# Cross attention of the prompt in seven products a pair of tiles instead of eight

## The chip, the cores and the metric

The kernel runs on one core of one Trainium2 chip. The metric is the device time of one execution in microseconds (us), the median of several. TensorE is called PE here (PEld is its weight load), VectorE DVE, ScalarE ACT, GpSimd POOL and SyncE SP; the last issues most of the transfers.

## What is computed

One layer of a streaming encoder over a prompt of 2048 rows (16 tiles of 128 rows, 1024 columns) and a sample tile of 128 rows: a mixer (attention and convolution), cross attention into 256 memory tokens, and a feed-forward network (FFN). The change touches the cross attention of the prompt and what it hands to the FFN:

```
h = rmsnorm(x, g_mem_pre)
x = x + rmsnorm(memory_attention(h, mk, mv, w_mq, w_mo), g_mem_post)
h = rmsnorm(x, g_ffn_pre)

def memory_attention(h, mk, mv, w_mq, w_mo):
    q = (h @ w_mq).reshape(B, T, MEM_HEADS, MEM_HEAD_DIM)
    s = einsum("bthd,bmhd->bhtm", q, mk) * MEM_HEAD_DIM ** -0.5
    p = softmax(s, axis=-1)
    o = einsum("bhtm,bmhd->bthd", p, mv).reshape(B, T, D_MODEL)
    return o @ w_mo
```

For the prompt, the memory is the same for all rows, so an earlier stage has multiplied the weights and the memory together: `f1s` (1024 x 1024) takes a normed row straight to its 4 x 256 scores, and `f2s` (1024 x 1024) takes its 4 x 256 probabilities straight to the 1024 columns of the output.

Every product is made in three matmuls of a split format: high x high, high x low and low x high, the high part a cast by ACT to fp32r and the low part the difference, by DVE or POOL.

## The kernel before

The stages run one after the other: the memory's products, the mixer's projections, its attention, its output (`mixout`, with the sample tile's cross attention as filling work), the prompt's cross attention (`phase_cross`), gate and up of the FFN (`gate_up`), its down projection. Instructions are written out for all engines, and a scheduler that works on modelled times puts each engine's list in order, earlier code first where several are ready; `high_priority` moves code ahead and `issue_after` holds it behind another instruction. Each engine and each transfer queue then runs its list strictly in order and waits on semaphores.

On-chip memory is laid out by hand. `Region.at` and `Region.lay` give each named tile a list of places (in KB) in three arenas: `sbF` (fp32), `sbR` (fp32r, its last 20 KB appear as sbx in the profile) and `ps` (PSUM), which live for the whole program; calling for a tile again takes the next place in its list. The `flex` tiles (flexb) are taken per stage, from memory that the stage ahead has given back.

`phase_cross` before: for each of 16 tiles, `norm` loads x1, makes 1/rms (ACT square, POOL power), scales (DVE, L317), transposes eight pieces on PE (L320) and splits them (ACT L321, DVE L322). `scores` multiplies them by f1: eight pieces of 128, each six matmuls of 128 x 512 (`mm3h`, L293: three forms by two halves of the 1024 columns). Softmax reads the scores in PSUM (DVE L1282, ACT L1286, DVE L1291), `probs` transposes and splits the probabilities (PE L1297, ACT L1300, DVE L1301), and `values` multiplies them by f2 in the same way. Score tile t+1 is computed between `probs` of t and `values` of t. `postnorm` (ACT L310, DVE L341, POOL L342) adds the residual and stores x2 (POOL's queue, L343). f1 and f2 (eight pieces of 1024 columns each, in high and low parts) lie on chip side by side, loaded and split by `load` (L1261, ACT L1264, DVE or POOL L1265).

The FFN multiplies pairs of tiles by the seven-product scheme of Strassen and Winograd. `natural` prepares its left side for a pair: it loads the two x2 tiles back, norms each, makes four combinations of their halves on POOL (L1330 to L1336) and stores seven pieces to `hn` by POOL's queue. One pair is done after each tile from the fifth on, and the last one inside `gate_up`. `gate_up` starts by loading `hn` pieces of its first six tiles, transposing and splitting them (`tform`: SP L1404, PE L1407, ACT L1409, DVE L1410) and by loading and combining the first weights (`wforms`: SP L1416 and L1417, POOL L1424 to L1427, ACT L1429, DVE L1430); both have `high_priority`. Its products are L285 to L287 (`mm3`), 384 rows a matmul.

## Time and profile before

| | before |
|---|---|
| median of 3 runs | 3001.84 us (2998.27 to 3007.77) |
| the profiled execution | 3001.3 us, its span 2999.5 us |
| mean granted TensorE clock | 0.992 |
| busy: PE, DVE, ACT, POOL | 98%, 71%, 45%, 47% of the span |

The profile is of one execution. The page gives each engine's busy time; the other views are answers about the same trace. In a timeline row stand the start and the duration in us, the engine, the line of the kernel, the operation, what it writes and reads, the shape and the count of equal instructions merged; in brackets the idle time before it and what ended it. In a row of groups stand the count, the busy time, the mean ns of one, the idle time before them and its releasers. A row of a source gives the smallest, median and largest ns. In a row by stretch stand the window, its length, then for PE, PEld, DVE, ACT and POOL the busy time and the count, then the granted clock, the busy share of the DMA engines and GB/s. SPq is SP's queue.

### The profile page before, as it was taken

Reading aid. Unit: us, or ns where it says so; the run is one execution under the profiler, and the core shown is the slowest. Engines: PE = TensorE matmul, PEld = TensorE weight load, DVE = VectorE, ACT = ScalarE, POOL = GpSimd, SP = SyncE. Lnnn points to the kernel's source line nnn. Section 1 sums busy time; section 2 is a strip of 40 time slices with the busy share of each in tenths; the row PEclk is TensorE's granted clock in tenths of the full one; section 3 lists DMA queues with packets and bytes.
Section 4 is the critical chain, followed back from the end, with each engine's and each line's share of the span. In section 5 each row is a group of like instructions: output and inputs, shape, how many; then the busy total and the mean of one; then the engine's idle time right before and its main releaser. Section 6 shows DMA issues by size and latency. Waiting matters only on the chain.

```text
span 2999.5 us, 46097 instructions
## 1 busy us (share of the span) xinstructions
PE 2939.8 (98%) x16924; PEld 2710.8 (90%) x16924; DVE 2134.7 (71%) x3086; ACT 1357.9 (45%) x2729; POOL 1419.3 (47%) x1338
## 2 busy tenths in 40 slices
PE   7999999989999999999999999999999999999998
PEld 7999999989998887887888999999999999888887
DVE  6697795877786466435358888888788998555666
ACT  4545364667884344323234333433334444433433
POOL 1268396731123335235357565555555775524413
PEclk9999999989999999999999999999999999999999
DMA  8735253655444556314246333544334345756664
GB/s 285 256 114 173 98 162 113 207 195 182 160 146 165 178 189 207 122 69 143 96 152 229 120 137 113 195 161 156 136 131 155 140 144 195 256 186 206 221 230 149
DMA packets 197694, 500.09 MB, mean 167 GB/s; under 512 B 19349, under 2 KB 84765, under 8 KB 188627
## 3 DMA queue, kind: packets, MB, share of 16 engines
q1 hardware_dynamic: 182539, 427.53, 42.0%
q0 software_dynamic: 14928, 69.61, 6.2%
q8 instruction: 133, 2.18, 0.3%
q14 instruction: 94, 0.77, 0.1%
HBM read 365.97 MB, written 141.81 MB: 169 GB/s over the span
## 4 chain that ended last, share of the span: by engine, by line
PE 38%; DMA 3%; DVE 3%; issue 3%; POOL 2%; ACT 1%; SPq 0%; DVEq 0%; POOLq 0%; ACTq 0%
PE psb L287 12%; PE psb L286 12%; PE psb L285 12%; DMA sbf<-in_w_down_dram 2%; PE psb L293 2%; POOL sbf L1552 1%; DMA sbf<-x 1%; PE psb L1407 1%; DVE sbr L1622 0%; DMA sbf<-hn 0%; DVE sbr L1430 0%; DVE sbr L1556 0%; POOL sbf L342 0%; DVE sbx L1430 0%; DVE flexb L1492 0%
## 5 line engine op out<-in xcount | busy, mean ns | idle before, releaser
L285 PE MATMUL psb<-sbr 128*128 128x384 f32 (+3 forms) x2808 | 942.4, 337 | 4.8 <-DVE flexb L430 2.1
L286 PE MATMUL psb<-sbr 128*128 128x384 f32 (+3 forms) x2356 | 807.1, 343 | 3.6 <-DVE sbr L322 3.3
L287 PE MATMUL psb<-sbr 128*128 128x512 f32 (+3 forms) x1848 | 633.2, 344 | 3.5 <-DVE sbr L1622 3.4
L285 PEld LDWEIGHTS psb<-sbr 128*128 128x128 f32 x2808 | 531.1, 189 | 34.7 <-DVE flexb L430 2.9
L287 PE MATMUL psb<-sbr,sbx 128*128 128x384 f32 (+2 forms) x1484 | 477.9, 323 | 0.0
L286 PEld LDWEIGHTS psb<-sbr 128*128 128x128 f32 x2356 | 446.0, 189 | 30.5 <-DVE sbr L322 3.6
L287 PEld LDWEIGHTS psb<-sbr 128*128 128x128 f32 x1848 | 348.1, 189 | 33.4 <-DVE sbr L1622 6.4
L293 PE MATMUL psb<-sbr 128*128 128x512 f32 x1200 | 295.0, 394 | 3.6 <-DVE flexb L1060 1.9
L1430 DVE TENSOR_TENSOR sbr<-sbf,sbr 128x512 fp32r<-128x512 f32 x258 | 262.4, 1020 | 39.9 <-ACT sbr L1429 39.1
L1429 ACT CAST sbr<-sbf 128x512 fp32r<-128x512 f32 x258 | 159.2, 620 | 279.1 <-PE psb L286 224.0
L287 PEld LDWEIGHTS psb<-sbr,sbx 128*128 128x128 f32 x1484 | 281.7, 190 | 0.2
L527 DVE SCALAR_TENSOR_TENSOR psb<-sbf,psb 128x768 f32<-128x768 f32 (+1 forms) x290 | 264.5, 912 | 6.1
L293 PEld LDWEIGHTS psb<-sbr 128*128 128x128 f32 x1200 | 222.1, 189 | 49.0 <-DVE flexb L1060 2.3
L1622 DVE TENSOR_TENSOR sbr<-sbf,sbr 128x384 fp32r<-128x384 f32 (+2 forms) x242 | 168.9, 721 | 96.1 <-ACT sbr L1621 93.5
L280 POOL TENSOR_TENSOR sbx<-sbf,sbr 128x1024 fp32r<-128x1024 f32 x62 | 157.6, 2545 | 78.3 <-ACT sbr L279 74.7
L1621 ACT CAST sbr<-sbf 128x384 fp32r<-128x384 f32 (+2 forms) x242 | 112.5, 483 | 171.6 <-PE psb L286 148.0
L1552 POOL TENSOR_TENSOR sbf<-sbf 128x512 f32<-128x512 f32 x77 | 106.9, 1392 | 166.6 <-DMA sbf<-in_w_down_dram 164.6
L537 POOL TENSOR_TENSOR flexb<-flexb,flexb 128x128 f32<-128x128 f32 (+1 forms) x180 | 169.2, 941 | 22.4 <-ACT flexb L536 11.8
L285 PE MATMUL psb<-sbr,sbx 128*128 128x384 f32 (+1 forms) x524 | 170.6, 327 | 0.7 <-ACT sbr L1409 0.7
L1429 ACT CAST sbx<-sbf 128x512 fp32r<-128x512 f32 x153 | 94.7, 620 | 160.8 <-PE psb L286 145.9
L1430 DVE TENSOR_TENSOR sbx<-sbf,sbx 128x512 fp32r<-128x512 f32 x153 | 154.9, 1014 | 15.1 <-ACT sbx L1429 14.8
L1424 POOL TENSOR_TENSOR sbf<-sbf 128x512 f32<-128x512 f32 x66 | 97.6, 1479 | 107.6 <-DVE sbr L1430 50.7
(345 smaller groups left out, 6257.4 us busy)
## 6 DMA issues: line engine op xcount, KB each, us to landing
af<-flexb SPq DMA_DIRECT2D x33, 1344.0 KB, 5.6
sbf<-in_w_down_dram SPq DMA_DIRECT2D x154, 256.0 KB, 3.5
sbf<-in_w_gate_dram SPq DMA_DIRECT2D x66, 512.0 KB, 3.3
sbf<-in_w_up_dram SPq DMA_DIRECT2D x66, 512.0 KB, 3.6
sbf<-af SPq DMA_DIRECT2D x85, 384.0 KB, 4.0
sbf<-x SPq DMA_DIRECT2D x49, 512.0 KB, 3.9
sbf<-in_w_in_dram SPq DMA_DIRECT2D x48, 512.0 KB, 4.0
sbr<-ks POOLq DMA_DIRECT2D x16, 1024.0 KB, 9.2
```

Source lines behind the costliest of these rows:

```text
L280: self.lo_engine.tensor_tensor(lo[:, :], wf[:, :], hi[:, :].bitcast(F32), ALU.subtract)
L285: nc.tensor.matmul(ps, lh, rh, start=start, stop=False, **kw)
L286: nc.tensor.matmul(ps, lh, rl, start=False, stop=False, **kw)
L287: nc.tensor.matmul(ps, ll, rh, start=False, stop=stop, **kw)
L293: nc.tensor.matmul(y[o], l, r[:, o * 512:(o + 1) * 512], start=start and x == 0, stop=stop and x == 2)
L527: nc.vector.scalar_tensor_tensor(acc if w < CW - 1 else o, src(w), cwt[:, j, w:w + 1], acc, ALU.mult, ALU.add)
L537: nc.gpsimd.tensor_tensor(o, o, v, ALU.add)
L1429: nc.scalar.copy(hs[j][:, :], src[j])
L1430: nc.vector.tensor_tensor(ls[j][:, :], src[j], hs[j][:, :].bitcast(F32), ALU.subtract)
L1552: nc.gpsimd.tensor_tensor(acc[:, :], acc[:, :], q[:, :], ALU.add if s > 0 else ALU.subtract)
L1621: nc.scalar.copy(ch[:, m], a[:, x, m])
L1622: nc.vector.tensor_tensor(cl[:, m], a[:, x, m], ch[:, m].bitcast(F32), ALU.subtract)
```

## The change

`phase_cross` is written anew, with the seven-product scheme for the cross attention too. The prompt's 16 tiles make eight pairs (the pairs that the FFN uses). There are 16 passes: eight over the pairs with f1 (scores), then eight with f2 (values). A pass is four rounds, one for each piece of 128 of the contracted half; a round makes seven products of three matmuls of 128 x 512 each, into seven PSUM banks that collect over the four rounds. `left` brings a pair's two tiles: for the scores it loads and norms x1, for the values it loads the probabilities, which the score passes now store in memory (`zs`). `turned` transposes four pieces for a round two rounds ahead, makes four small combinations (128 x 128), and splits seven pieces at once (896 columns) into `row`, a flex tile. `side` loads the two halves of f1 or f2 for one round's index, makes four combinations and splits seven pieces. There is room for one factor alone: f2 replaces f1 piece by piece during the eighth pass. `collect` evicts the seven banks into two tiles by one ACT copy and seven DVE additions.

After a score pass, softmax runs on the collected tiles, its scaling on POOL. After a value pass, `residual` norms and adds x1 (loaded a second time) and stores x2 for the end of the kernel; then `ffn_norm` and `natural` make the FFN's combinations straight from the tiles on chip, and their stores go through SP's queue. The sample pair is done at the start of the fourth pass (round 12); nothing is left for `gate_up`. In `mixout` two small areas change places (`sh`).

```diff
+        pool = (Region().lay(sbF, 0, ("g", 4, 2), ("z", 4, 4), ("ft", 2, 4)).lay(sbF, 0, ("g", 4, 2), ("y", 4, 4), ("x1", 4, 2))
...
+                .at("row", 7, *[(rows[i], [0]) for i in (1, 2, 3, 0)]))
...
+        ps_mm = ps_t = Region().at("mm", 2, (self.ps, [0, 2, 4, 6, 8, 10, 12])).at("t", 2, (self.ps, [14]))
...
+        def side(src, k):
...
+            b11, b12, b21, b22 = raw
+            t1, t3, t2, t4 = [self.t(pool, [P, 512], F32, "ft")[:, :] for _ in range(4)]
+            ptt(t1, b12, b11, ALU.subtract)
+            ptt(t3, b22, b12, ALU.subtract)
+            tt(t2, b22, t1, ALU.subtract)
+            tt(t4, t2, b21, ALU.subtract)
+            out = {}
+            for i, (j, x) in enumerate(((0, b11), (4, t1), (2, b21), (6, b22), (3, t3), (1, t2), (5, t4))):
+                hi = self.t(pool, [P, 512], F32R, f"fh{k}{i}")[:, :]
+                nc.scalar.copy(hi, x)
+                lo = self.t(pool, [P, 512], F32R, f"fl{k}{i}")[:, :]
+                tt(lo, x, hi.bitcast(F32), ALU.subtract)
+                out[j] = (hi, lo)
+            return out
...
+        def turned(ab, k, q):
...
+            pt = self.t(ps_t, [P, 4, P], F32, "t")
+            for i, (x, kk) in enumerate(((b, k), (a, k), (a, k + 4), (b, k + 4))):
+                nc.tensor.transpose(pt[:, i, :], x[:, kk * P:(kk + 1) * P], self.ident[:, :])
+            g = self.t(pool, [P, 8, P], F32, "g")
+            nc.scalar.copy(g[:, :4, :], pt[:, :, :])
+            b0, a0, a1, b1, s1, s2, s3, s4 = (g[:, i, :] for i in range(8))
+            other = ptt if q < 8 else tt
+            ptt(s1, b0, b1, ALU.add)
+            other(s3, a0, b0, ALU.subtract)
+            ptt(s2, s1, a0, ALU.subtract)
+            other(s4, a1, s2, ALU.subtract)
+            row = self.t(pool, [P, 14, P], F32R, "row")
+            nc.scalar.copy(row[:, :7, :], g[:, 1:, :])
+            tt(row[:, 7:, :], g[:, 1:, :], row[:, :7, :].bitcast(F32), ALU.subtract)
...
+        def collect(ps, tag):
...
+            nc.scalar.copy(a0, ps[0])
+            tt(a1, a0, ps[1], ALU.add)
+            tt(b0, a1, ps[3], ALU.add)
+            tt(b1, b0, ps[4], ALU.add)
+            tt(a1, a1, ps[4], ALU.add)
+            tt(b0, b0, ps[5], ALU.subtract)
+            tt(a1, a1, ps[6], ALU.add)
+            tt(a0, a0, ps[2], ALU.add)
...
+            for h in range(MH):
+                nc.gpsimd.tensor_scalar(zv[:, h, :], zv[:, h, :], ri[:, h:h + 1], None, ALU.mult)
+            nc.gpsimd.dma_start(self.zs[t], z)
...
+        def residual(t, y, x1):
+            r = rstd(y)
+            stt(y, y, r[:, :], self.gpost[:, :], ALU.mult, ALU.mult)
+            ptt(y, y, x1[:, :], ALU.add)
+            nc.gpsimd.dma_start(self.x2[t], y)
+
+        def ffn_norm(src, dst, n=P):
+            r = rstd(src, n)
+            stt(dst, src, r[:n, :], gffn[:n, :], ALU.mult, ALU.mult)
+
+        def natural(dst, xa, xb, n=P):
...
+            ptt(u[:, 0, :], xb[:, 0, :], xa[:, 0, :], ALU.subtract)
+            nc.sync.dma_start(dst[:n, 0:2, :], xa)
+            ptt(u[:, 1, :], xb[:, 1, :], u[:, 0, :], ALU.subtract)
+            nc.sync.dma_start(dst[:n, 4:6, :], u)
+            ptt(xb[:, 0, :], xb[:, 1, :], xb[:, 0, :], ALU.subtract)
+            nc.sync.dma_start(dst[:n, 2:4, :], xb)
+            ptt(xa[:, 1, :], u[:, 1, :], xa[:, 1, :], ALU.subtract)
+            nc.sync.dma_start(dst[:n, 6, :], xa[:, 1, :])
...
+        def finish(q, ps):
+            ta, tb, g, p = pairs[q % 8]
+            if q < 8:
+                for t, z in zip((ta, tb), collect(ps, "z")):
+                    softmax(t, z)
+                return
...
+            for t in (ta, tb):
+                x1 = self.t(pool, [P, D], F32, "x1")
+                nc.sync.dma_start(x1[:, :], self.x1[t])
...
+            ys = collect(ps, "y")
+            for t, y, x in zip((ta, tb), ys, xs):
+                residual(t, y, x)
+                ffn_norm(y, x)
+            natural(self.hn[g][:, p, :, :], *xs)
...
+        for r in range(n):
+            q, k = divmod(r, 4)
+            if k == 0:
+                ps = [self.t(ps_mm, [P, 512], F32, "mm")[:, :] for _ in range(7)]
+                if q + 1 < 16:
+                    nat[q + 1] = left(q + 1)
+            if r + AHEAD < n:
+                x, kk = divmod(r + AHEAD, 4)
+                acts[r + AHEAD] = turned(nat[x], kk, x)
+            act = acts.pop(r)
+            for j in (0, 2, 6, 4, 3, 1, 5) if r == 0 else (0, 1, 3, 4, 5, 6, 2):
+                self.mm3(ps[j], *act[j], *f[k][j], k == 0, k == 3)
+            if q == 7:
+                f[k] = side(f2, k)
+                if k == 3:
+                    self.gpost = self.gain(pool, "g_mem_post", "gain")
+            if k == 3:
+                finish(q, ps)
+            if r == 12:
+                samples()
...
-                    if g == 0 and x == 1 and self.todo:
-                        self.natural(*self.todo.pop(0))
```

199 lines of the change are left out of this document (81 added, 118 removed).

## The prediction

> **What bounds the kernel now.** I read the page first, then the busy time by stretch, then the timeline of TensorE through the stage that changes.
>
> ```profile
> span 2999.5 us, 46097 instructions
> PE 2939.8 (98%) x16924; PEld 2710.8 (90%) x16924; DVE 2134.7 (71%) x3086; ACT 1357.9 (45%) x2729; POOL 1419.3 (47%) x1338
> ...
> 1196.00:1582.00 386.00, 379.55 (x1792) 314.50 (x1791) 179.96 (x194) 126.23 (x266) 154.51 (x180) 1.00 0.34 119
> ```
>
> TensorE (PE) is busy for 98% of the span. In the cross attention of the prompt (1196 to 1582) it stands idle for about 6 of 386 us, while VectorE (DVE), ScalarE (ACT) and GpSimd (POOL) are at 47%, 33% and 40%. Matmuls taken away there shorten the time as long as the other three can do what is put on them instead.
>
> ```profile
> 1190.52 1.20 PE L293 MATMUL psb<-flexb,sbx 128*128 128x512 f32 x4 [0.77 <-DVE flexb L1085]
> 1194.97 1.80 PE L320 MATMUL psb<-ident,sbf 128*128 128x128 f32 x8 [3.25 <-DVE sbr L322]
> 1196.42 7.62 PE L293 MATMUL psb<-sbr 128*128 128x512 f32 x28
> ...
> 1258.97 8.87 PE L293 MATMUL psb<-sbr 128*128 128x512 f32 x38
> ...
> 1566.63 1.03 PE L1297 MATMUL psb<-ident,sbf 128*128 128x128 f32 x8
> 1567.42 2.09 PE L293 MATMUL psb<-flexb,sbr 128*128 128x512 f32 x8
> ...
> 1582.14 0.34 PE L285 MATMUL psb<-sbr 128*128 128x384 f32 x1
> ```
>
> The last sample matmul ends near 1191.7, the first score product starts at 1196.42 and the first gate/up product at 1582.14. Inside, 38 matmuls take 8.87 us: (8.87 - 0.39) / 37 = 0.229 us from one to the next. Eight transposes take 1567.42 - 1566.63 = 0.79.
>
> **The change, part by part.** The profiled execution took 3001.3 us (1.8 around the span) and the median of the runs is 3001.84; the sum is made against 3001.3.
>
> *Matmuls.* Before: 16 tiles x 2 products x 8 pieces x 6 = 1536. After: 64 rounds x 7 products x 3 = 1344. The transposes stay 256. 192 x 0.229 = 44.0 us less. A round is 21 x 0.229 + 4 x 0.099 = 5.2 us, and a pass of four rounds over one pair of tiles 20.8.
>
> *Prices*, from sources and groups:
>
> ```profile
> L537 POOL TENSOR_TENSOR flexb<-flexb,flexb x180: 453/462/2842, 198.7 to 620.7; 128x128 f32<-128x128 f32 x120, 128x768 f32<-128x768 f32 x60
> L806 POOL TENSOR_SCALAR flexb<-flexb,flexb x4: 961/963/984, 665.9 to 863.6; 128x272 f32<-128x272 f32 x4
> L342 POOL TENSOR_TENSOR sbf<-sbf x16: 2380/2396/3412, 1241.6 to 1586.0; 128x1024 f32<-128x1024 f32 x16
> L1425 POOL TENSOR_TENSOR sbf<-sbf x66: 1282/1542/1777, 1554.2 to 2508.6; 128x512 f32<-128x512 f32 x66
> L303 POOL TENSOR_TENSOR sbf<-sbf,mhalf 128x1 f32<-128x1 f32 x28 | 15.5, 555 | 2.3
> L302 POOL TENSOR_SCALAR sbf<-sbf 128x1 f32<-128x1 f32 x28 | 5.2, 186 | 178.1 <-ACT sbf L310 178.1
> DMA to landing us min/median/max: 3.1/4.8/5.8
> L1430 DVE TENSOR_TENSOR sbr<-sbf,sbr x258: 676/693/1979, 1550.4 to 2520.6; 128x512 fp32r<-128x512 f32 x129
> L1265 DVE TENSOR_TENSOR flexb<-sbf,flexb x5: 1214/1226/1226, 1224.0 to 1233.2; 128x1024 fp32r<-128x1024 f32 x5
> L317 DVE SCALAR_TENSOR_TENSOR sbf<-sbf x16: 1271/1791/3389, 1167.0 to 1536.1; 128x1024 f32<-128x1024 f32 x16
> L1410 DVE TENSOR_TENSOR sbr<-psb,sbr 128x512 fp32r<-128x512 f32 x4 | 2.8, 690 | 6.8 <-ACT sbr L1409 6.8
> L1429 ACT CAST sbr<-sbf x258: 602/622/627, 1548.9 to 2520.0; 128x512 fp32r<-128x512 f32 x129
> ```
>
> The smallest or median durations are the undisturbed ones. VectorE between 512 and 1024 columns gains 1.05 ns a column: 0.27 for 128, 1.09 for the 896 of the low parts.
>
> *The start.* The split combinations (`row`) and the gains lie in the flex tiles, in memory that the mixer's output stage held.
>
> ```profile
> 1191.76 1.02 ACT L310 ACTIVATE flexb<-psb 128x1024 bf16<-128x1024 f32 x1 [1.60 <-PE psb L293]
> ...
> 1205.61 1.27 DVE L341 SCALAR_TENSOR_TENSOR flexb<-psb,flexb 128x1024 f32<-128x1024 f32 x1
> ...
> 1210.57 0.63 POOL L343 DMA_DIRECT2D x<-flexb  x1 [0.30 <-POOL flexb L342]
> ...
> 1214.03 0.33 SPq L364 DMA_DIRECT2D flexb<-in_g_ffn_pre_dram  x1
> ```
>
> The load of g_ffn_pre comes ahead of all f1 loads in the program, yet starts at 1214.03, 3.5 us after the sample's last store from that memory was issued: a flex tile is given over whole. Before, no score product touched one. After, the first needs `row`, and its transposes need a PSUM bank that holds the sample's y until L341. The shortest chain, from the square at 1191.76: 1.0, then 0.74 for 1/rms (L302, L303), 1.3 (L341), 2.4 (L342), 0.9 for issuing, 3.1 to land (the least of L343's), 0.9 for the copy into `row` (896 columns, between 0.62 for 512 and the square's 1.02 for 1024): 1202.1, or 6 later than 1196.42. Before lost 7.62 - 28 x 0.229 = 1.2 in its first tile, where after has its weights ready for two rounds. I take +5; if L341 runs as late as now the first product comes at about 1215 and it is +17; 0 if the conversions of f1, which pace rounds 2 and 3 either way, swallow it.
>
> [...]
>
> ```profile
> 1699.22 1.47 POOL L1522 TENSOR_TENSOR flexb<-flexb 128x384 f32<-128x384 f32 x1
> 1700.66 1.28 POOL L1425 TENSOR_TENSOR sbf<-sbf 128x512 f32<-128x512 f32 x1
> 1701.91 1.74 POOL L1426 TENSOR_TENSOR sbf<-sbf 128x512 f32<-128x512 f32 x1
> ...
> 1700.38 0.55 DVE L1483 TENSOR_TENSOR sbf<-sbf,psb 128x384 f32<-128x384 f32 x1
> 1700.85 1.65 DVE L1430 TENSOR_TENSOR sbr<-sbf,sbr 128x512 fp32r<-128x512 f32 x1
> 1702.42 1.65 DVE L1485 SCALAR_TENSOR_TENSOR flexb<-flexb,sbf 128x384 f32<-128x384 f32 x1
> ```
>
> L1483, with one operand in PSUM, runs its 0.55 beside L1522. L1430, with both inputs in SBUF, starts beside L1425 and ends 0.56 after it (2.50 against 1.94); L1426 then ends 1.15 after L1430. They take turns; only some 0.13 us of each, its issue, overlaps.
>
> [...]
>
> Score passes: POOL 16 combinations x 0.46 + 8 scalings x 0.91 (L806, at 256 columns) = 14.6; DVE with two SBUF inputs 4 x 1.09 + 2 x 1.27 = 6.9. Together 21.5 by durations, 17.6 by turns (0.13 off each of 30), of 20.8. So it fits, narrowly; the four `z` tiles give a lag of two passes. +2 (0 to 6).
>
> Value passes: POOL 8 x 0.46 + 2 residual additions x 2.39 + 4 FFN combinations x 1.28 = 13.6; DVE 4 x 1.09 + 8 x 0.27 + 4 x 1.27 = 11.6. Together 25.2 by durations and 21.3 by turns, of 20.8. POOL's own list adds four 1/rms (0.74 each) and two stores; its FFN stores move to SP, behind loads that wait for their slots. Four `y` tiles let the finishing of a pair lag by two passes, but the gate/up stage needs the space of the last `y` and `x1`, so the lag is paid at the latest there. I take 22.0 a pass, nearer to the turns, since L1430 shows turns: 7 passes x 1.2 = +8 (3 to 31).
>
> For scale, gate/up runs close to this:
>
> ```profile
> 1700.00:1900.00 200.00, 200.00 (x1155) 200.00 (x1155) 162.19 (x221) 76.56 (x139) 114.38 (x82) 1.00 0.36 128
> ```
>
> There DVE and POOL together are busy 277 of 200 us, blocked time included, and PE stands still for none of it.
>
> *The change from f1 to f2.* Four sides in rounds 29 to 35 (7 x 5.2 = 36 us). DVE: 36 x 0.69 = 24.8, low parts 7 x 1.09 = 7.6, evictions 7 x 0.69 = 4.8 (L1410's form), two maxima over 1024 columns (some 1.2 each) and six small differences: 4, an estimate: 41. ACT: 28 x 0.62 = 17.4 and its usual work, which fits. DVE is 5 over: +6 (0 to 16, with POOL's 8 x 1.28 on the port).
>
> *Into gate/up.*
>
> ```profile
> 1586.56 0.66 PE L1407 MATMUL psb<-ident,sbf 128*128 128x128 f32 x4 [0.55 <-DVE sbr L1410]
> 1590.10 1.25 PE L1407 MATMUL psb<-ident,sbf 128*128 128x128 f32 x8 [0.97 <-DVE sbr L1410]
> 1596.47 1.16 PE L1407 MATMUL psb<-ident,sbf 128*128 128x128 f32 x8 [1.73 <-DMA sbf<-hn]
> ...
> 1597.00:1602.00 5.00, 4.67 (x19) 4.04 (x19) 1.57 (x3) 1.27 (x3) 4.98 (x6) 0.66 0.74 193
> ...
> sbf<-in_w_up_dram SPq DMA_DIRECT2D x66, 512.0 KB, 3.6
> ```
>
> Before waits 3.3 us in these three, since first loads and conversions were done earlier. After, the first w_up load goes to the space of the last pair's `y`, and the first gate/up sum to its `x1`. From the last cross product: the last evictions 2, two squares 2.0, 1/rms 0.7, scaling 1.3, two additions 4.8, square and 1/rms 1.8, scaling 1.3, four combinations 5.1, store 3.1, two gate/up sums 2.6, cast 0.6: product 1 can start 25 us on. PE has products 0 and 2 (24 x 200 / 1155 = 4.2) and 84 transposes (8.3) till then: 13 idle, so +10 (0 to 20). Each such pause also costs clock: 0.66 was granted at 1597 to 1602, after the waits. [...]
>
> Sum: -44 + 5 + 2 + 6 + 8 + 10 = -13: **2988 us**.
>
> **Rivals.**
> *The cover holds.* `z`, `y` and AHEAD = 2 soak up the lag, and the last pair finishes beside the 21 transposed loads of gate/up: -44 + 5 + 2 + 3 = -34, 2967 us. For it: VectorE, ScalarE and GpSimd each stay under 20.8 a pass alone, and gate/up above. Against: the turns.
> *The port becomes the bound* (slower). Turns as costly as whole durations, 25.2 a pass: -44 + 5 + 6 + 10 + 7 x 4.4 + 10 = +18, 3019 us (6 and 10 for the score passes and f2, toward their upper ends). It also needs only GpSimd's order going wrong, 2.4 us additions ahead of 0.46 us combinations that PE waits for. It decides from 23.8 a pass, where the sum is nil. For it: 21.3 is already over 20.8. Against: two passes of slack.
> *The matmuls saved aren't worth it*: seven banks in turn might pace worse than 0.229.
>
> ```profile
> L285 PE MATMUL psb<-sbr 128*128 128x512 f32 x692 | 270.0, 390 | 0.0
> L293 PE MATMUL psb<-sbr 128*128 128x512 f32 x764 | 185.0, 393 | 1.7 <-ACT sbr L1300 1.1 <-POOL sbr L1265 0.6
> ```
>
> The seven-product form in the down stage (L285) takes 390 ns, as the pairs do (393); at 0.25 it would be 2988 + 1344 x 0.02 = 3015.
>
> **How the numbers follow.** About 0.3% (9 us) can be told from no change. The forecast 0.45, its own range 2973 to 3009 (faster 0.25, same 0.20); the cover holds 0.20, faster; the port 0.31 (slower 0.28, same 0.03); the pace 0.04 (slower 0.03, same 0.01). Faster 0.45, same 0.24, slower 0.31. Range 2962 to 3026, from the cover's price less 5 to the port's and 8 more.
>
> **What would show it.** Right: 1344 matmuls at 0.229; first product at about 1202; value passes near 22 us; POOL near 90% from the ninth pass on, with its additions and VectorE's two-input instructions above 2.4 and 1.3; a pause of 10 to 20 us ahead of gate/up's second product, ended by POOL or a load. Wrong: passes at 20.8 and no pause (the cover), passes of 24 or more with PE waiting for `row` or for evictions (the port).

## The result, and the profile after

The changed kernel takes 3156.43 us (median of 4, 3153.48 to 3160.00) where the kernel before takes 3004.81 beside it: 1.0506 times the time, 95% interval 1.0488 to 1.0524. It is slower by 152 us; 2988 had been forecast and 2962 to 3026 given as the range.

The head of the page, the stretches of the stage (busy time of PE, PEld, DVE, ACT and POOL, then granted clock, DMA share and GB/s) and TensorE's rows around them, all of the changed kernel:

```profile
span 3155.9 us, 46575 instructions
PE 2935.6 (93%) x16732; PEld 2693.6 (85%) x16732; DVE 2276.3 (72%) x3289; ACT 1445.1 (46%) x2881; POOL 1610.4 (51%) x1587
```
```profile
1213.00:1460.00 247.00, 190.06 (x800) 151.43 (x800) 138.43 (x172) 111.60 (x244) 166.97 (x237) 0.87 0.25 87
1460.00:1667.00 207.00, 182.12 (x788) 143.70 (x788) 143.56 (x177) 76.97 (x130) 137.82 (x153) 0.94 0.38 142
1667.00:1733.00 66.00, 3.16 (x13) 2.36 (x13) 23.18 (x22) 16.12 (x28) 40.37 (x41) 0.54 0.44 163
```
```profile
1213.01 0.79 PE L285 MATMUL psb<-sbr,flexb 128*128 128x512 f32 x1 [9.91 <-ACT flexb L1330]
...
1666.52 0.39 PE L287 MATMUL psb<-sbr,flexb 128*128 128x512 f32 x1
1684.43 1.12 PE L1475 MATMUL psb<-ident,sbf 128*128 128x128 f32 x4 [17.52 <-DVE sbf L1344]
1730.28 1.97 PE L1475 MATMUL psb<-ident,sbf 128*128 128x128 f32 x8 [44.74 <-DMA sbf<-hn]
1732.93 0.69 PE L285 MATMUL psb<-sbr 128*128 128x384 f32 x1 [0.68 <-ACT sbr L1477]
```

Before, TensorE was full in this stage; now no engine is. Four pieces make the 156.4 us between the two spans (3155.9 and 2999.5): the first product starts at 1213.0 for 1196.4 (+16.6); the passes take 453.7 where the stage before took 385.7 (+68.0); between the last product and the first of gate/up TensorE pauses for 66.2 us, where before there was no pause (the three waits of 3.3 us came just behind the first gate/up product); from that product on it takes 1422.9 for 1417.4 (+5.5).

For every kernel below I took the starts of the 1344 products with 512 columns (84 to a pass) and of the first gate/up product. A pass lasts from its first product to that of the next; passes 1 to 7 make scores, f2 replaces f1 in the eighth, and passes 9 to 16 make values. In us:

| kernel | ratio | first product | passes 1–7, mean | 8 | 9 | 10–16, mean | pause | gate/up on |
|---|---|---|---|---|---|---|---|---|
| after | 1.0506 | 1213.0 | 29.4 | 41.5 | 30.1 | 25.2 | 66.2 | 1422.9 |
| e1 x1 free | 1.0425 | 1219.7 | 28.7 | 41.5 | 29.2 | 25.8 | 34.9 | 1429.6 |
| e2 scaling on DVE | 1.0351 | 1218.0 | 23.1 | 33.7 | 26.6 | 24.6 | 67.6 | 1427.4 |
| e3 operands first | 1.0467 | 1221.9 | 28.9 | 38.0 | 25.9 | 23.8 | 67.1 | 1423.8 |
| e4 e1+e2+e3 | 1.0254 | 1224.8 | 22.6 | 28.8 | 32.9 | 25.4 | 35.0 | 1430.3 |
| e6 places | 1.0485 | 1219.1 | 28.6 | 41.3 | 29.7 | 25.2 | 20.5 | 1461.4 |
| e7 sums on DVE | 1.0358 | 1217.0 | 23.9 | 32.0 | 30.1 | 25.1 | 60.9 | 1425.7 |
| e8 same, from PSUM | 1.0357 | 1215.6 | 26.1 | 38.0 | 28.7 | 25.5 | 42.2 | 1428.7 |
| e9 finishing order | 1.0401 | 1214.0 | 28.7 | 41.4 | 29.7 | 25.3 | 26.3 | 1436.6 |
| e10 e9+e1+e2 | 1.0269 | 1213.2 | 23.2 | 33.4 | 26.5 | 28.0 | 21.1 | 1435.7 |
| e11 addition on DVE | 1.0173 | 1217.5 | 23.0 | 33.6 | 26.7 | 23.7 | 25.2 | 1427.2 |
| e12 scaling dealt out | 1.0410 | 1221.1 | 25.2 | 32.2 | 31.9 | 24.9 | 66.5 | 1426.7 |
| e13 | 1.0197 | 1215.5 | 23.2 | 37.4 | 30.3 | 24.4 | 16.3 | 1429.0 |
| e14 | 1.0148 | 1214.4 | 21.5 | 33.3 | 27.0 | 23.9 | 13.7 | 1438.1 |
| e15 | 1.0141 | 1210.1 | 22.0 | 39.6 | 25.8 | 22.4 | 16.3 | 1441.6 |
| e16 | 1.0143 | 1216.3 | 22.0 | 39.9 | 27.4 | 21.5 | 11.5 | 1454.1 |
| e17 no FFN sums | 1.0306 | 1220.3 | 28.6 | 41.2 | 29.7 | 22.3 | 15.9 | 1428.1 |
| e18 e15, no FFN sums | 1.0073 | 1211.6 | 22.2 | 40.1 | 25.8 | 20.9 | 7.2 | 1441.1 |

The ratios' 95% intervals reach 0.0013 to 0.0018 to either side. They are taken against the kernel before as it ran beside each (3004.0 to 3009.0 us), so small differences are read from them and not from the times. All runs but e5 are in the table.

### The profile page after: what moved, and what is told of

The parts are those of the page before. It is cut to its first block, busy times and chain, and to the rows that moved or that the text cites. A ratio compares the mean times of both kernels' runs of the same rounds, so it can differ in the third digit from the quotient of the medians.

```text
span 3155.9 us, 46575 instructions
## 1 busy us (share of the span) xinstructions
PE 2935.6 (93%) x16732; PEld 2693.6 (85%) x16732; DVE 2276.3 (72%) x3289; ACT 1445.1 (46%) x2881; POOL 1610.4 (51%) x1587
## 4 chain that ended last, share of the span: by engine, by line
PE 40%; POOL 3%; DMA 3%; issue 2%; DVE 1%; ACT 1%; POOLq 0%; SPq 0%; DVEq 0%; ACTq 0%
PE psb L287 13%; PE psb L286 13%; PE psb L285 13%; DMA sbf<-in_w_down_dram 1%; POOL sbf L1618 1%; PE psb L1475 1%; DMA sbf<-x 1%; DMA sbf<-hn 1%; POOL sbf L1364 0%; ACT sbf L1295 0%; DVE sbr L1688 0%; POOL sbf L1297 0%; POOL flexb L1377 0%; POOL sbf L1298 0%; DMA hn<-sbf 0%
## 5 line engine op out<-in xcount | busy, mean ns | idle before, releaser
L285 PEld LDWEIGHTS psb<-sbr 128*128 128x128 f32 x2808 | 530.3, 189 | 35.0 <-ACT sbr L1687 1.9
L286 PEld LDWEIGHTS psb<-sbr 128*128 128x128 f32 x2356 | 445.2, 189 | 29.7 <-DVE sbr L322 3.6
L287 PEld LDWEIGHTS psb<-sbr 128*128 128x128 f32 x1848 | 347.9, 189 | 32.9 <-DVE sbr L1688 6.1
L285 PE MATMUL psb<-sbr,flexb 128*128 128x512 f32 (+2 forms) x496 | 194.6, 392 | 66.2 <-ACT flexb L1330 63.6
L286 PE MATMUL psb<-sbr,flexb 128*128 128x512 f32 (+2 forms) x532 | 211.8, 398 | 0.0
L1618 POOL TENSOR_TENSOR sbf<-sbf 128x512 f32<-128x512 f32 x77 | 106.6, 1390 | 166.4 <-DMA sbf<-in_w_down_dram 164.8
L287 PE MATMUL psb<-sbr,flexb 128*128 128x512 f32 (+2 forms) x496 | 171.9, 374 | 4.9 <-DVE flexb L1331 4.8
L285 PEld LDWEIGHTS psb<-sbr,flexb 128*128 128x128 f32 x496 | 98.0, 198 | 84.9 <-ACT flexb L1330 68.6
```

The costliest lines, as they stand in the source:

```text
L285: nc.tensor.matmul(ps, lh, rh, start=start, stop=False, **kw)
L286: nc.tensor.matmul(ps, lh, rl, start=False, stop=False, **kw)
L287: nc.tensor.matmul(ps, ll, rh, start=False, stop=stop, **kw)
L1618: nc.gpsimd.tensor_tensor(acc[:, :], acc[:, :], q[:, :], ALU.add if s > 0 else ALU.subtract)
```

## The experiments

Two readings are set against each other. By the *lists*, what costs is the order of each engine's list: a short instruction that TensorE needs stands behind long ones. By the *port*, what costs is the sum of the durations of VectorE's instructions with two SBUF inputs and of GpSimd's, as if they had to run one after the other. The port, in the prediction and the expectations too, is a name for what these instructions wait for; what it is, no run shows. What the prediction's rows show is that they get longer beside each other: L1430 took 1.65 us beside L1425 and L1426, where its shortest took 0.68.

**Score passes: where the scalings stand.** GpSimd in the fourth pass of the changed kernel, and TensorE's wait there:

```profile
1304.88 0.46 POOL L1328 TENSOR_TENSOR sbf<-sbf 128x128 f32<-128x128 f32 x1
1308.61 7.26 POOL L1358 TENSOR_SCALAR sbf<-sbf 128x256 f32<-128x256 f32 x8 [3.27 <-DVE sbf L1356]
1315.83 0.46 POOL L1325 TENSOR_TENSOR sbf<-sbf 128x128 f32<-128x128 f32 x1
...
1322.04 1.84 POOL L1328 TENSOR_TENSOR sbf<-sbf 128x128 f32<-128x128 f32 x2
```
```profile
1324.49 0.80 PE L285 MATMUL psb<-sbr,flexb 128*128 128x512 f32 x1 [6.42 <-ACT flexb L1330]
```

GpSimd stands idle 3.3 us ahead of the scalings (their exponentials aren't done), scales for 7.3 us, and only then makes the combinations of the next rounds: 17 us from one round's L1328 to those of the next two rounds. Two rounds of lookahead are 10.4 us.

e2 takes the scalings out of that list:

```diff
-                nc.gpsimd.tensor_scalar(zv[:, h, :], zv[:, h, :], ri[:, h:h + 1], None, ALU.mult)
+                nc.vector.tensor_scalar(zv[:, h, :], zv[:, h, :], ri[:, h:h + 1], None, ALU.mult)
```


> Edit: the eight scalings of a pair's softmax (L1358, 0.9 us each on GpSimd) go to VectorE, one line. Theory of the lists: GpSimd works off its list in its written order, and the scalings (7.3 us in a row) stand there ahead of the combinations of the next rounds that TensorE waits for; with them gone from that list the score passes, 23 to 41 us now (mean 30.9 of eight), lose 3 to 6 us each from the third on: about 25 us less, 3130 us, and the combinations L1325 to L1328 of a round follow each other at once. Port theory: the same direction, by 7.3 us of the port a pass less what VectorE's scalings cost there, also some 20 to 30 us; so the two are told apart by e3, and this run only gives the price of the scalings. If neither holds and operands come late for another reason (x1 loads and 1/rms of the next pair), under 10 us are won.

3113.07 us: 43 less, and the passes not touched by f1's conversions or the samples run at 20.6 to 21.2. That fits list and port alike. e5 and e12 keep the scalings on GpSimd and deal them out, two to a round:

```diff
+                late.append(lambda h=h: nc.gpsimd.tensor_scalar(...))        # e5, e12
...
+            with self.tc.issue_after(self.last_comb.ins):                    # e12 alone: behind L1327
+                for _ in range(min(2, len(late))):
+                    late.pop(0)()
```


> Edit: the softmax scalings stay on GpSimd, as many and as long as before, but are written two to a round into the four rounds of the next pass, behind that round's combinations, instead of sixteen... eight after another per tile at the end of a pass. Moving them to VectorE won 43 us (ratio 1.035 for 1.051) and brought the score passes from 30.9 to 24.4 us in the mean. Theory of the lists: what costs is that combinations stand behind a block of scalings that itself waits for the exponentials (GpSimd idled up to 7.6 us ahead of a block in e1); dealt out, they cost little: score passes of 22 to 25 us, 3115 to 3130 us in all. Port theory: the work on the shared port is the same, 21.5 us by durations a pass, so the score passes stay near 29 to 31 and the time within 12 us of 3156.

e5 took 3159.68: the scheduler put the scalings in rows of eight as before (1311.24, 7.24 us, x8), so it tests nothing.

> Edit: what e5 meant to do and did not (its list of GpSimd came out with the eight scalings of a pair in a row as before, so e5 says nothing): here two scalings are made to follow a round's combination on GpSimd. Engines, work and durations are those of the changed kernel. Theory of the lists: score passes from 30.9 in the mean to 22 to 25, 3110 to 3130 us in all, near e2. Port theory: 21.5 us of port work a pass by durations as before, score passes above 28, time within 12 us of 3156.

e12 took 3131.49, 25 us less, with the same work on the same engines; passes 1 to 7 fell from 29.4 to 25.2 in the mean, pass 8 from 41.5 to 32.2. TensorE's longest waits in passes 3 to 7 (us, times, longest), in the changed kernel, e12 and e2:

```profile
PE psb L285 <- ACT flexb L1330: 30.0, 6, 8.5
...
PE psb L285 <- ACT flexb L1330: 15.4, 8, 4.5
...
PE psb L285 <- ACT flexb L1330: 6.3, 2, 3.3
```

L1330 is the cast of the split combinations. So most of what e2 won is the order of GpSimd's list; the 2 us a pass between e12 and e2 may be the port's or the list's. In pass 8 the block of scalings took even longer:

```profile
1436.63 11.19 POOL L1358 TENSOR_SCALAR sbf<-sbf 128x256 f32<-128x256 f32 x8
```

The combinations behind it came to GpSimd at 1447.8; the last one of the round (L1328, in VectorE's list) stood there behind f2's sums, low parts and evictions until 1458.7, and TensorE waited 12.1 us for the cast after it.

e3 only asks for another order:

```diff
+                    with self.tc.high_priority(offset=200):
                         nat[q + 1] = left(q + 1)
...
+                with self.tc.high_priority(offset=200):
                     acts[r + AHEAD] = turned(nat[x], kk, x)
```


> Edit: what makes the operands of coming rounds (the transposes with copy, combinations and split; and the loading and norm of the next pair) gets a higher priority (200 steps of the program) when the order of each engine's list is written; no work is added, moved to another engine or left out. Theory of the lists: the score passes get shorter, since combinations no longer stand behind scalings and squares of finished tiles: 20 to 40 us less, 3115 to 3135. The value passes stay, as the ring of the x1 tiles sets them. Port theory: the sum of the work on the port is the same, so the time stays within 10 us of 3156.

3147.84, 9 us less: not the list theory's 20 to 40, and within the 10 that the port theory allowed. But the scheduler takes whatever is ready first by its modelled times, and six of the eight blocks of eight scalings stayed whole in the list, so e3 does not decide between the two.

**The port by itself.** e7 and e8 differ in where VectorE reads:

```diff
-            ptt(s1, b0, b1, ALU.add)
+            tt(s1, b0, b1, ALU.add)                     # e7; s2, s3 and s4 likewise
+            tt(s1, pt[:, 0, :], b1, ALU.add)            # e8: one input from PSUM; s2, s3 and s4 likewise
```


> Edit: all four combinations of a round (L1325 to L1328) on VectorE, reading from SBUF as before: 0.27 us instead of 0.46 each, and none in GpSimd's list. This run and e8 are a pair: the lists of all engines are of the same kind in both, only the port differs. Port, by durations: a score pass 7.3 (scalings) + 11.2 (VectorE with two SBUF inputs) = 18.5 us; a value pass 9.9 + 13.8 = 23.7 us. Port theory: value passes stay at 24 or more, since TensorE needs 20.8. Theory of the lists: GpSimd's finishing work stands ahead of nothing that TensorE waits for; score passes 21 to 23, value passes 21 to 23, and some 60 to 90 us won: 3065 to 3095.

> Edit: as e7, but each of the four combinations takes one of its two inputs from PSUM, where the transposes left it, so that (as the one-PSUM-input evictions in the trace of before ran beside GpSimd) it need not take turns with GpSimd. Port, by durations: a score pass 14.2 us, a value pass 9.9 + 9.5 = 19.4 us. Port theory: value passes fall to 21 to 22, by 2 to 3 us each below e7, so 15 to 25 us less than e7. Theory of the lists: the same as e7 within 10 us.

3113.88 and 3113.03. In e7 the value passes stayed at 25.1, as the port theory said and the list theory (21 to 23) did not. In e8, where the port theory has them at 21 to 22, they are 25.5: the port's sum of durations does not bound these passes. The equal times hide two differences. e8's score passes are 2 us longer: 9.1 us of TensorE's waits in them end on its L1327, the last combination, which in e8 reads the one PSUM bank that the next transposes need; e7 has no such wait. And e8's pause is 18.7 us shorter, so a pair's finishing did go faster with less work on the port.

**The pause is a debt.** GpSimd's residual addition of each pair at the end of the stage:

```profile
1664.59 2.39 POOL L1364 TENSOR_TENSOR sbf<-sbf 128x1024 f32<-128x1024 f32 x1 [7.50 <-DMA sbf<-x]
...
1692.38 2.34 POOL L1364 TENSOR_TENSOR sbf<-sbf 128x1024 f32<-128x1024 f32 x1 [7.53 <-DMA sbf<-x]
...
1719.91 2.34 POOL L1364 TENSOR_TENSOR sbf<-sbf 128x1024 f32<-128x1024 f32 x1 [6.42 <-DMA sbf<-x]
```

Each row is the first addition of a pair. It waits for an x1 load, which waits for the x1 tile, which the FFN norm fills and the last of four stores gives back: 27.5 to 27.8 us a pair, all in one chain, against 20.8 for a pass. The last three passes (27.1, 27.7, 27.5) run at that period, and after the last product three pairs are still owed.

```diff
-                ffn_norm(y, x)                          # e1: the norm over y, x1 free after the addition
-            natural(self.hn[g][:, p, :, :], *xs)
+                ffn_norm(y, y)
+            natural(self.hn[g][:, p, :, :], *ys)
```


> Edit: the FFN norm of a value tile is written over y itself instead of over its x1 tile, so an x1 tile is free after the residual addition and no longer held until the four stores of the FFN combinations have landed. The work on every engine stays the same. Ring theory: in the changed kernel the residual addition (L1364) of a new pair starts every 27.5 to 27.8 us at the end of the stage, after a reload of x1 (4.2 to 5.1 us) that waits for the stores of the pair before; the value passes take on this period (27.1 to 27.7 us for the last three) and the finished pairs still owed make the 66 us pause after the last cross product. Without the ring the passes from the third value pass on fall to 21 to 23 us (some 25 us less in all) and the pause to 20 to 30 us (some 40 less): about 3090 us, ratio 1.03 to the kernel before, against 1.051. Port theory: what VectorE and GpSimd share is as full as before, so value passes stay at 25 or more and at most 15 us are won: 3140 or more.

```diff
             for t, y, x in zip((ta, tb), ys, xs):       # e9: both residuals, then both norms
                 residual(t, y, x)
-                ffn_norm(y, x)
+            for y, x in zip(ys, xs):
+                ffn_norm(y, x)
```


> Edit: the finishing of a pair of value tiles is written in another order, nothing else: first both residuals, then both FFN norms (before: residual and norm of one tile, then of the other). GpSimd's list then has the two residual additions next to each other, and ScalarE's squares of the second tile no longer stand behind the addition of the first. Theory of the finishing chain: a pair is finished in a chain of 27.7 us (from one L1364 to that of the next pair: 1664.59, 1692.38, 1719.91 in the changed kernel), longer than a pass needs (20.8), so each value pass comes to wait for the y tiles of two passes ago, and the debt of some three pairs is the 66 us pause. By the same rows the new chain is: reload 5, two additions 4.8, square 1.2, 1/rms 1.6, scaling 1.3, combinations 6, store 2.1 = 22 us. Value passes then fall from 25.8 to 22 to 23 (some 22 us less), the pause by 10 to 30: 3105 to 3125 us. Port theory: same work, same port: within 12 us of 3156.

e1: 3135.71; e9: 3129.23. Both cut the pause (to 34.9 and 26.3), as the chain theory says; neither shortened the value passes (25.8 and 25.3), which by the same theory should have fallen to 21 to 23. So the chain sets the debt; it is not alone in setting the passes. 7 and 14 us of the gain come back in gate/up. What TensorE waits for shows why. In the last seven passes of the changed kernel:

```profile
PE psb L285 <- DVE sbf L1340: 4.2, 3, 2.5
PE psb L285 <- DVE sbf L1339: 3.6, 2, 2.8
PE psb L1320 <- ACT sbf L1322: 3.5, 2, 3.0
PE psb L285 <- ACT sbf L1338: 2.6, 1, 2.6
PE psb L287 <- DVE flexb L1331: 2.5, 1, 2.5
PE psb L285 <- ACT flexb L1330: 2.2, 3, 1.1
PE psb L285 <- DVE sbf L1345: 1.6, 1, 1.6
```

12.0 of these 20.2 us end on evictions (L1338 to L1345), which free the seven banks for the next pass, and 8.2 on operands (L1322, L1330, L1331). In e9 it is 3.9 us on evictions and 16.5 on operands: one wait was exchanged for the other, and the passes stayed.

e6 changes only places, so that gate/up's first loads need not wait for the last pair:

```diff
-            w = wforms(0)
+            w = wforms(0, "0")                          # tiles wf0, s0, nat0 in places that are free early
```


> Edit: only places in memory: gate/up's first weights, sums and transposed loads go to where the last pair of the cross attention holds nothing (g, the z tiles loaded last), its first output tile and the PSUM bank of its first transposes as well. The data that the first gate/up products need (the FFN combinations of the first three pairs) is there long before. Theory of the places: the 66 us pause is the time that the last pairs' finishing holds these places; now it falls to 5 to 20 us, and since the finishing then runs beside gate/up, some of it comes back there (gate/up keeps VectorE and GpSimd full by itself): 25 to 50 us won, 3105 to 3130. Rival: the pause is set by the lists or by SP's queue, in which the loads stand behind the last stores of the combinations, each waiting for GpSimd: then the pause stays above 45 and under 15 us are won.

3151.62. The pause fell to 20.5, and 38.5 us came back after it: the debt is paid beside gate/up's first products, in the same lists. TensorE's longest waits from 1687 to 1760 (us, times, longest):

```profile
PE psb L1476 <- DMA sbf<-hn: 17.2, 5, 12.1
PE psb L285 <- ACT sbf L1535: 11.3, 1, 11.3
```

**Together.** 

> The edits of e1, e2 and e3 together. If ring and lists are the whole of it and add up: score passes of 22 to 25 us, value passes of 21 to 23, a pause of 20 to 30 us: 3156 - 65 - 45 = about 3045, some 1.5% above the kernel before. Port theory: the scalings' 7.3 us a pass are the only relief, 3125 or more.

3082.31, neither 3045 nor 3125 or more: the score passes and the pause fell, the value passes (25.4) did not move.

```diff
-            ptt(y, y, x1[:, :], ALU.add)
+            tt(y, y, x1[:, :], ALU.add)                 # e11: e10 with this
```


> Edits: e9's order, e1's (norm written over y, x1 tile free after the addition) and e2's (scalings on VectorE). Theory of the finishing chain: with both, two pairs can be finished at a time, so the chain no longer sets the passes; value passes 21 to 23, pause 20 to 30: from e2's 3113, 20 us in the passes and 30 in the pause less, 3055 to 3070, 1.6 to 2.2% above the kernel before. If the parts of the port set the value passes (25.2 us by durations), they stay at 24 to 26 and 3085 or more results.

> Edit: e10, and the residual addition on VectorE (1.23 us where GpSimd takes 2.39). The finishing chain of a pair shortens by 2 to 3 us, the port's work by 2.3 us a pass, VectorE gets 2.5 us more a pass (19 of 20.8). Chain theory: passes as in e10 or 1 us less, pause 4 us shorter: 3045 to 3060. Port theory: value passes fall by 2 us from e10's.

3089.80 and 3060.22. In e10 the two additions of a pair stand close together in GpSimd's list, and the value passes grow to 28.0; 25.9 us of TensorE's waits in the last seven end on the cast L1330. (In e9 the additions stand together too, and its passes are 25.3; what makes the difference is not shown.) GpSimd, then TensorE, in e10:

```profile
1472.39 0.46 POOL L1325 TENSOR_TENSOR sbf<-sbf 128x128 f32<-128x128 f32 x1
1472.81 3.32 POOL L1364 TENSOR_TENSOR sbf<-sbf 128x1024 f32<-128x1024 f32 x1
1476.10 1.31 POOL L1381 TENSOR_TENSOR sbf<-flexb,sbf 128x512 f32<-128x512 f32 x1
1477.37 0.45 POOL L1327 TENSOR_TENSOR sbf<-sbf 128x128 f32<-128x128 f32 x1
```
```profile
1481.34 0.79 PE L285 MATMUL psb<-sbr,flexb 128*128 128x512 f32 x1 [7.06 <-ACT flexb L1330]
```

L1327 needs L1325, half a microsecond of work, and starts 5.0 us after it, behind an addition and a sum; TensorE waits 7.1 us. Off GpSimd, the same additions let the passes fall to 23.7, by more than either theory's 1 or 2 us.

**Start, samples, f2.** e13 takes VectorE's two combinations of a value round from PSUM, orders the `row` tiles `(2, 3, 1, 0)` and puts f2's sums t2 and t4 on GpSimd; e14 has e6's places, the same `row` order, and the samples' sums after the last pass:

```diff
+                tt(s3, a0, pt[:, 0, :], ALU.subtract)            # e13, q >= 8
+                tt(s4, pt[:, 2, :], s2, ALU.subtract)
+            sums = ptt if src is f2 else tt                      # e13, in side
+                .at("row", 7, *[(rows[i], [0]) for i in (2, 3, 1, 0)]))      # both
-            if r == 12:                                          # e14
-                samples()
+        samples()
```


> Base: e11 (1.0173 to the kernel before). Three edits that lie in different stretches of the trace and are read there. (a) In the value passes VectorE's two combinations of a round (L1326, L1328) take one input from PSUM: same lists, but by durations the port's work falls from 23.0 to 20.8 us a pass. Port theory: value passes fall from 23.7 (mean of the last seven) to 21 to 22. If lists or latency hold them, they stay within 0.7 of 23.7. (b) The `row` tiles are used in another order, so that the first two lie in memory that the mixer's last normalisations don't hold. Theory of the start: the first product starts at 1197 to 1205 in place of 1213 to 1217, and the change of e11's start, 20 us over the kernel before, halves. Rival: it was the order of ScalarE's and VectorE's conversions of f1: stays at 1210 or later. (c) The sums t2 and t4 of f2's factors go to GpSimd: VectorE has 8 x 0.69 = 5.5 us less in the two passes of the change to f2, 33.6 and 26.7 us now; if VectorE's list sets them, they lose 3 to 6 us together. In all 3030 to 3050.

> Base: e11. Three edits in different stretches. (a) The places of e6 (gate/up's first tiles where the last pair holds nothing). In e6 the pause fell from 66 to 20 and 38 us came back in gate/up, since the finishing debt of three pairs stayed. In e11 the pause is 25 with a smaller debt. Theory of the debt: pause 5 to 10, and 5 to 15 us of it come back in gate/up (the rest from the first gate/up product on goes from 1427 to 1430 to 1440). (b) The FFN combinations of the samples are made after the last pass, not in the fourth. Theory of the lists: the fourth pass, 30.5 us in e11 beside 20.6 to 21.2 of its neighbours, falls to 21 to 23, as their four sums of 1.28 us on GpSimd and squares on ScalarE stood ahead of combinations; 8 to 10 us won there, 2 to 6 of them lost at the end. (c) The `row` tiles as in e13. In all 3025 to 3045.

3062.58 and 3047.06. Less port work in the value passes: 24.4 for 23.7, the port theory's second miss. `row`: first product at 1215.5 and 1214.4, where e11 has 1217.5 and the changed kernel 1213.0, not 1205 or earlier. f2's sums on GpSimd: passes 8 and 9 longer by 7.4. The samples: pass 4 fell from 30.5 to 20.9. The places: pause 13.7 for 25.2, 10.9 back in gate/up, in both of which the samples' sums now stand too.

e15 puts the combinations of passes 8 and 9 on VectorE and the first pair's x, the gain and f1's sums in memory that is free earlier; e16 is e15 with the FFN sums of the last five pairs and the samples made later, in gate/up:

```diff
+            some = tt if q in (7, 8) else ptt                    # e15, for s1 and s2
+            .at("gain", 4, (sbF, [24, 42.5])).at("x0", 4, (sbF, [8, 12]))
+            if g > 0:                                            # e16
+                self.todo.append((g, p))                # made from x2 in gate/up's first group
+                return
```


> Base: e14 (1.0148). Two edits in different stretches. (a) In the two passes of the change to f2 the combinations of a round are all on VectorE. In e14 one combination of 0.46 us on GpSimd (L1325 at 1384.22) ended only after 7.25 us, when a run of twelve VectorE instructions with two SBUF inputs, without a break between them, had ended, and TensorE then stood still for 8.2 us. Theory: GpSimd gets the port only when VectorE's run breaks, it does not take turns; so without GpSimd's combinations that pause goes, and the two passes, 33.3 and 27.0 us now, lose 6 to 12 us together though VectorE has 4 us more to do. Rival: VectorE's sum of work sets these passes: they stay or grow by 1 to 4 us. (b) The first pair's x tiles, the gain and the sums of f1 lie where the mixer's last weights are not (they are held until about 1185), f1's loads use two places instead of four. Theory of the start: L1309 and so the first transposes, at 1201 in e14, move to before 1193, the first product to 1199 to 1206 from 1214. Rival: ScalarE's and VectorE's conversions of f1 set it, which are not earlier: 1212 or later. In all 3025 to 3038 by both theories, 3040 to 3050 by both rivals.

> Base: e15. Edit: only the first three pairs' FFN combinations (group 0) are made from the residuals on chip; those of the other five pairs and of the samples are made one after another in gate/up's first group from x2, as the kernel before did with what it had left. Theory of density: the kernel before spread a pair's finishing (two 1/rms and scalings each, additions, four sums of 1.28 us) over 48 us of TensorE, the changed one has to do all of it in the 20.8 us of a value pass; the lists and the port get as full as in gate/up, but here the operands of the next 10 us hang on them. With less of it the value passes from the fourth on fall from 24 to 25 to 21 to 22.5 (some 12 us), the pause from 14 to 5 to 8, and gate/up, which is full but has long lookahead, pays 0 to 10: 3005 to 3025. Rival (VectorE's and ScalarE's own work of collecting and splitting sets the passes): within 6 us of e15.

3049.31 and 3052.10. e15: the first transposes came at 1194.22, 7 us earlier than in e14, the first product only 4. TensorE's, ScalarE's and GpSimd's rows:

```profile
1194.22 1.12 PE L1321 MATMUL psb<-ident,sbf 128*128 128x128 f32 x4 [4.81 <-DVE flexb L341]
...
1210.14 0.80 PE L285 MATMUL psb<-sbr,flexb 128*128 128x512 f32 x1 [6.17 <-ACT flexb L1332]
```
```profile
1197.05 0.58 ACT L1323 COPY sbf<-psb 128x512 f32<-128x512 f32 x1
```
```profile
1195.58 3.27 POOL L342 TENSOR_TENSOR flexb<-flexb 128x1024 f32<-128x1024 f32 x1
...
1206.55 1.71 POOL L1280 TENSOR_TENSOR sbf<-sbf 128x512 f32<-128x512 f32 x1
1208.22 1.76 POOL L1330 TENSOR_TENSOR sbf<-sbf 128x128 f32<-128x128 f32 x2
```

The transposed blocks were there at 1197.6. Behind the sample's addition and one of f1's sums, GpSimd began the first combination at 1201.7; the fourth (the first of the two in the last row) ended at 1209.1, and the cast L1332 started at once. So in e15 GpSimd's list holds the start; what part of it is order, and what part sums that took 0.9 to 1.4 us for 0.46, is not told apart.

Passes 8 and 9 took 65.4 for 60.3, so (a) missed: one of f2's sums on GpSimd (L1281) now took 6.09 us where L1325 had taken 7.25. e16: passes 13 to 16 ran at 21.0, 20.6, 21.3 and 20.6, so it is the FFN part of the finishing work that holds the value passes; and gate/up took 12.5 us more, where passes and pause had won 9.6.

**What the second part costs.** e17 and e18 leave out the FFN norm and the four FFN sums of a pair and store the residuals themselves, from `ys`, so that gate/up works on other numbers in the same way; in e17 the x1 tiles also come free after the addition, as in e1:

```diff
-                ffn_norm(y, x)
-            natural(self.hn[g][:, p, :, :], *xs)
+            plain(self.hn[g][:, p, :, :], *ys)
```

> Base: the changed kernel. Left out: the FFN norm and the four FFN sums of the value passes; the residuals themselves are stored in the sums' place, by the same stores, so gate/up computes on other data in the same time. This prices the second part of the change (FFN combinations from the residuals on chip) in its own kernel. If it is what holds the value passes and makes the debt: the last seven value passes fall from 25.2 to 21 to 22 (some 25 us), the pause from 66 to 10 to 20 (some 50): 3075 to 3090, and about half of the 155 us is left for the first part (the score passes, the start, the change to f2). Rival: residuals, collecting and splitting alone fill the value passes: 24 or more, pause above 35, 3110 or more.

> Base: e15 (1.0141), with the same left out as in e17. What is left against the kernel before is the cost of the form itself: start 14, the change to f2, the last pair's residual ahead of gate/up. Value passes 20.6 to 21.5 (now 22.4), pause 4 to 10 (now 16), the rest from the first gate/up product on 1420 to 1428 (now 1442): 3005 to 3020. If it ends below 2995, the FFN sums are all that stands between the form and a gain; above 3025, gate/up's slower beginning has another cause than this work.

e17: 3096.87, 60 us less than the changed kernel: pause 15.9, value passes 22.3. e18: 3028.32, still 1.0073 (1.0060 to 1.0086) times the kernel before. Its passes take 367.8, 18 less than the stage before, 20.9 each in the last seven; but it starts 15 us later, pauses 7, and needs 24 more from the first gate/up product on, most of it in the first 100 us there (464 matmuls, where the kernel before has 547). By the forecast a time above 3025, which this only just is, means that gate/up's slower beginning has another cause than the FFN sums. No kernel here beats the one before.

## Why the prediction was wrong

By its own terms, with 20.8 us for a pass without waits:

| term | predicted | measured |
|---|---|---|
| matmuls | 192 fewer; a pass 20.8 | 1344; 20.6 to 20.9 where nothing waits |
| start | +5 (0 to 17) | +16.6 |
| score passes (1–7) | +2 (0 to 6) | 7 x 8.6 = +60 |
| to f2 (passes 8, 9) | +6 (0 to 16) | 71.6 - 41.6 = +30 |
| value passes (10–16) | +8 (3 to 31) | 7 x 4.4 = +31 |
| into gate/up | +10 (0 to 20) | +66, and 5.5 after it |

With -44 for the matmuls the rows add up to 165, 9 more than the spans' 156: the stage before itself held 9 us (385.7 - 1536 x 0.229 - 256 x 0.099) that passes of 20.8 do not have.

*Right:* the count and the pace of the matmuls (the third rival falls), and that the debt is paid at the handover.

*The step that failed* is "it fits, narrowly; the four `z` tiles give a lag of two passes". The sum of durations on the port was compared with 20.8 us, and tiles were taken as the slack. But tiles let only the finishing lag. Combinations and finishing share one list, and in it an instruction that waits, or a block of 7.3 us, holds back half a microsecond that TensorE needs within 10.4 us (e2, e12, e10): +60 us in the score passes where +2 was forecast, 29 of them gone by order alone in e12. The rival named this, "GpSimd's order going wrong", without working out a price. GpSimd was not near 90% busy from the ninth pass on, as the prediction had it, but at 67% (137.82 of 207 us): no engine was full.

*The port rival* met its condition, passes above 23.8 us, and its 25.2 us a value pass is the 25.2 measured; yet the sum of durations is not what sets it, as e8 and e13 took port work away and the passes stayed (25.5 and 24.4 us, for 25.1 in e7 and 23.7 in e11). That number was luck, and its whole price, 3019, is 137 us short. That these instructions hold each other up for whole durations, on which the price rests, no run shows; what the runs show is the overlap of some 0.13 us that the prediction reads from its rows, and in e14 a wait far longer than one instruction (7.25 us for 0.46). (By its own rule, 3019 and 8 more, the range ends at 3027 and not 3026; nothing hangs on it.)

*The handover:* one pair's chain of 25 us was priced, and 27.5 is what a pair takes. That such chains follow each other without overlap, in a ring of two x1 tiles, one pair per 27.5 us against 20.8 for a pass, was missed; three pairs were owed, not one. So the lag of two passes did not come free either: the evictions that TensorE waits for in the value passes stand among this finishing.

*The change to f2* was summed on VectorE alone. Of the +30, 16 us are waits in pass 8 for operands, 12.1 of them for a round that GpSimd's scalings (11.19 us) and then VectorE's list held back; e2 and e12 shortened that pass by 8 and 9.

*The start* came out at the end of its range, but not by the release of the flex tile, as I argued:

```profile
1200.73 0.63 POOL L343 DMA_DIRECT2D x<-flexb  x1
```
```profile
1206.57 0.33 SPq L364 DMA_DIRECT2D flexb<-in_g_ffn_pre_dram  x1
```
```profile
1210.00 0.94 DVE L1282 TENSOR_TENSOR sbf<-sbf 128x512 f32<-128x512 f32 x1
```
```profile
1210.97 1.14 ACT L1286 CAST sbr<-sbf 128x512 fp32r<-128x512 f32 x2 [1.48 <-DVE sbf L1282]
1212.02 1.77 ACT L1330 CAST flexb<-sbf 128x896 fp32r<-128x896 f32 x2
```

The store was issued at 1200.73 and landed 5.8 us later; the load of g_ffn_pre into a flex tile started at 1206.57. The first round's combinations ended at 1204.3. But the copy into `row` stood behind f1's casts, which waited for f1's load and for VectorE's sums, until 1212. The rows are GpSimd's, SyncE's, VectorE's and ScalarE's of the changed kernel.

*Left out altogether:* the clock within passes. Two stretches of the changed kernel after the wait at 1324.49, columns as above:

```profile
1324.50:1330.80 6.30, 6.30 (x15) 4.96 (x16) 3.15 (x3) 2.30 (x3) 1.86 (x4) 0.51 0.01 3
1332.90:1342.90 10.00, 10.00 (x48) 8.18 (x48) 7.03 (x11) 6.94 (x21) 6.43 (x11) 1.00 0.29 105
```

15 matmuls in 6.3 us at a clock of 0.51, then 48 in 10.0 at full clock. In the passes of the changed kernel 120 starts follow the one before by 0.36 to 0.55 us; at 0.229 each they would have taken 24 us less. Another 89 of the 121 us lost are the 38 intervals longer than that. The rest are starts 0.30 to 0.36 apart, mostly behind transposes, and passes without waits have four of these too.

Still open: what of the finishing work holds the value passes at 22 to 24 us in e11, e14 and e15. Neither the port's sum nor the chain alone does it; TensorE's waits there end in part on evictions (5.4 of 12.2 us, 8.0 of 11.7, 3.8 of 7.3), and whether these are late by VectorE's list or by the `y` tiles no run tells. Open as well: the rest of the change to f2, and what share of e18's 24 us in gate/up its new places cause.

## What to carry to other kernels

A sum of durations per engine says only that a stage could keep up. Ask for each short instruction that the busy engine waits for what stands ahead of it in its own list, what that in turn waits for, and compare the delay with the lookahead. Then work out the period of each ring of buffers (load, use, store, reload) against a pass: a ring that is slower leaves a debt, and moving it beside a stage that is full gives the time back there (in e6 38.5 us of the 45.7 that the pause lost, in e16 12.5 for 9.6).

## What the runs showed of the hardware

In e14 GpSimd and VectorE did not take turns: one combination of 0.46 us took 7.25 us, while VectorE finished one instruction with two SBUF inputs and ran eleven more without a break between them:

```profile
1384.22 7.25 POOL L1325 TENSOR_TENSOR sbf<-sbf 128x128 f32<-128x128 f32 x1
```
```profile
1383.86 0.68 DVE L1288 TENSOR_TENSOR sbx<-flexb,sbr 128x512 fp32r<-128x512 f32 x1
1384.46 0.68 DVE L1288 TENSOR_TENSOR sbr<-sbf,sbr 128x512 fp32r<-128x512 f32 x1
1385.07 1.88 DVE L1288 TENSOR_TENSOR sbx<-sbf,sbr 128x512 fp32r<-128x512 f32 x3
1386.87 1.08 DVE L1331 TENSOR_TENSOR flexb<-sbf,flexb 128x896 fp32r<-128x896 f32 x1
1387.87 0.68 DVE L1282 TENSOR_TENSOR sbf<-sbf 128x512 f32<-128x512 f32 x1
1388.48 0.28 DVE L1326 TENSOR_TENSOR sbf<-sbf 128x128 f32<-128x128 f32 x1
1388.68 2.48 DVE L1288 TENSOR_TENSOR sbr<-sbf,sbr 128x512 fp32r<-128x512 f32 x4
1393.14 1.34 DVE L1328 TENSOR_TENSOR sbf<-sbf 128x128 f32<-128x128 f32 x1 [1.98 <-POOL sbf L1327]
```

It ended (1391.47) 0.3 us after VectorE's run did (1391.16). e2 and e11 show the same 7.25 us. By these rows the wait was for a whole run of instructions. What decides between such a wait and the turns that the prediction's rows show, no run here tells.

Pauses of 2 to 3 us already lowered the clock at times (21 of 47). I counted TensorE's pauses (from one start to the next) in the passes of the changed kernel and its 18 variants, where the 15 starts ahead followed each other within 0.36 us at full clock. The shortest stretch at half clock in these traces is 3.41 us (in the changed kernel at 0.50 from 1265.84 to 1269.25, say). Within that time of the pause's end, and before any other pause, the granted clock halved (0.5 in its record, 1.0 before) after none of 136 pauses of 0.6 to 2 us, 21 of 47 of 2 to 3 us, 31 of 42 of 3 to 4 us and all 45 of 4 us or more. The chances grow with the pause, and a pause of 2 to 3 us was no safe one here.
